# One level of Strassen's scheme in both down-projections of a hybrid decoder layer

## The chip, the core and the metric

The kernel runs on one core of one Trainium2 chip. The metric is device time in microseconds (us) of one execution, the median of several. Engines in the text: PE (TensorE, matmuls; PEld is its weight load), DVE (VectorE), ACT (ScalarE), POOL (GpSimd), SP (SyncE, which issues all the loads and stores here). SBUF is the on-chip memory, PSUM the eight accumulator banks that PE writes.

## What is computed

One decoder layer on 512 tokens of width 1024, in float32. The change lies in the two SwiGLU blocks ("macaron" half-steps), which stand at the start and near the end of the layer:

```
def swiglu(x, w_gu, w_down):
    g, u = jnp.split(x @ w_gu, 2, axis=-1)
    return (jax.nn.silu(g) * u) @ w_down
...
f = swiglu(rms_norm(h, ffn1_pre_g[i]), ffn1_w_gu[i], ffn1_w_down[i])
h = h + 0.5 * rms_norm(f, ffn1_post_g[i])
```

w_gu is 1024 x 5632, w_down 2816 x 1024. Between the blocks stand an attention stage (projection, two mixers, output projection), and after the second one a gate: h + norm(sigmoid(norm(h) @ W_gate) * (p @ W_ple)).

## The kernel before

Every matrix product runs in three terms. An operand X is split into a high part, rounded to the format that PE multiplies (fp32r), and a low part, X minus the high part: `nc.scalar.copy(hi, raw)` on ACT, then a subtraction on DVE (POOL for some weights in the attention stage). A product is then high x high, high x low, low x high: three matmuls of 128 x 128 by 128 x 512.

Stages in order: SwiGLU 1 (22 blocks of gate and up columns, `ffn`, then `down`), the value projection `v_b`, attention with the other projections filled in, the output projection `out_part`, SwiGLU 2, the gate. The order of PE's instructions is the order of the program text; the other engines' instructions are put in order by the planner, which keeps the program's dependencies; `tc.high_priority()` lifts some.

Weights go through a ring of slots (8 KB per partition each: 1024 columns high, 1024 low). `todo` is the list of weights to come, `free` the list of slots; `pump()` hands slots out, `prep` (L131 to L133) loads 512 KB into one of three raw buffers, casts and subtracts; `release(key)`, called where the last matmul on a weight stands, gives the slot back. Four slots lie in `WR`, and up to four more in parts of `HB` that are not written yet. `HB` holds the hidden activations, high and low, 22 blocks of 128 features by 512 tokens. `gu_evac` (L250 to L253) makes one block: silu on ACT, product on DVE, cast on ACT, subtraction on DVE.

`down` goes over 16 of the 22 feature blocks for all four token tiles, 6 matmuls each, and then over the last 6 blocks tile by tile (`M_LAST`), so that tile 0 ends first and its `finish` (norm, residual, norm of the next stage: `post` and `pre`, L193 to L215) runs beside the matmuls of the others. `between(t)` puts the transposes of tiles 0 and 1 into the matmuls of tiles 2 and 3. `extra` prepares the first weights of the next stage (`vb` or `gate`).

Of the kernel before, what the change touches and what calls it, by code (L numbers as in the profile page):

```python
# [22 lines left out]
M_LAST = 6  # L23
# [30 lines left out]
def hybrid_layer(ctx: ExitStack, tc: tile.TileContext, x, p, rel_bias, ffn1_pre_g, ffn1_w_gu, ffn1_w_down,  # L54
# [4 lines left out]
    pool = ctx.enter_context(tc.tile_pool(name="sb", bufs=1))  # L59
    psp = ctx.enter_context(tc.tile_pool(name="ps", bufs=1, space=bass.MemoryType.PSUM))  # L60
# [11 lines left out]
    HB = sb([P, 2, NFF, 512], F32R, "hb")  # L72
    WR = sb([P, 8, 1024], F32R, "wr")
    RAW = sb([P, 3, 1024], F32, "raw")
    FB = sb([P, 7 * 1024], F32, "fb")
# [16 lines left out]
    def mm(o, l, r, start, stop):  # L92
        nc.tensor.matmul(o, l, r, start=start, stop=stop)  # L93
# [3 lines left out]

    def ht(u):
        return (HB[:, 0, 2 * u:2 * u + 2, :].rearrange("p a b -> p (a b)"),
                HB[:, 1, 2 * u:2 * u + 2, :].rearrange("p a b -> p (a b)"))  # L100

    ring = [(WR[:, 2 * i, :], WR[:, 2 * i + 1, :]) for i in range(4)]

# [4 lines left out]
    def source(key):  # L108
# [9 lines left out]
        w = {"d1": ffn1_w_down, "d2": ffn2_w_down, "o": w_out, "gate": w_ple_gate, "ple": w_ple_proj}[kind]  # L118
        return dram(w, i * P * D, [[D, P], [1, D]])

    def prep(key, slot):
        hi, lo = slot
        raw = RAW[:, state["raw"] % 3, :]
# [20 lines left out]
    def release(key):  # L144
        slot = W.pop(key)
        if not any(slot is r for r in retired):
            free.append(slot)
        pump()

# [22 lines left out]

    def flat(a):
        return a.rearrange("p a b -> p (a b)")
# [83 lines left out]
    def down_part(ffn, t, k, slot, w):  # L258
        cols = slice(t * P, (t + 1) * P)
        ps = slot2(slot)  # L260
        xstat([ps[:, 0, :], ps[:, 1, :]], HB[:, 0, k, cols], HB[:, 1, k, cols], w[0], w[1], k == 0, k == NFF - 1)

# [9 lines left out]
    todo += gu_list("1") + [("d1", k) for k in range(NFF)]  # L272


    ring_more = [(ht(7), 11), (ht(8), 13), (ht(9), 15), (ht(10), 17)]
    free.extend(a for a, _ in ring_more[:3])
    praw = FB[:, 6144:7168].rearrange("p (k t c) -> p k t c", k=2, t=NT)
    pT = ht(10)
# [65 lines left out]
    free.append(ring_more[3][0])  # L344
# [4 lines left out]
    def ffn(n, wait_tr, after_first, extra_slots):  # L349
# [7 lines left out]
        for ff in range(NFF):  # L357
            s = gu_slot(ff)
            for slot, until in extra_slots:
                if ff == until:  # L360
                    retired.append(slot)
                    free[:] = [a for a in free if a is not slot]
# [5 lines left out]

    def down(n, extra, finish, between):

        last = NFF - M_LAST
        for k in range(last):
            for t in range(NT):
                down_part(n, t, k, t, W[("d" + n, k)])
            if k == last - 4:
                free.extend([ht(0), ht(1)])
                retired.extend([free[-1], free[-2]])
            release(("d" + n, k))
        extra()
        for t in range(NT):  # L380
            for k in range(last, NFF):
                if k == NFF - 2 and t >= 2:
                    between(t)
                down_part(n, t, k, t, W[("d" + n, k)])
            if t == NT - 1:
                for k in range(last, NFF):
                    release(("d" + n, k))
            finish(t)

# [39 lines left out]
    ffn("1", tr_first, lambda: tables(gu_slot(8), gu_slot(9)), ring_more)  # L429
# [4 lines left out]
    def first_extra():  # L434
        for j in range(4):
            prep(("vb", j), ht(4 + j))
# [33 lines left out]
    VV = HB[:, :, 0:4, :]  # L470

    def vtile(t):
        return HB[:, t % 2, 2 * (t // 2):2 * (t // 2) + 2, :].rearrange("p a (h s c) -> p (a h) s c", s=2, c=64)
# [22 lines left out]
    v_b(0)  # L496
# [7 lines left out]
    MH, ML = HB[:, 0, 6:14, :], HB[:, 1, 6:14, :]  # L504
    VAT = HB[:, 0, 4:6, :].rearrange("p a (b g s c) -> p (a b) g s c", b=2, g=2, s=2)
# [3 lines left out]
    ptb2 = [HB[:, 1, 4, :], HB[:, 1, 5, :]]  # L509
# [4 lines left out]
    def tab(s):  # L514
        if s >= 4:
            return FB[:, 6144 + (s % 2) * 512:6656 + (s % 2) * 512]
        return FB[:, 6144:7168] if s % 2 == 0 else FB[:, 5120:6144]
# [281 lines left out]
    load_tab(5)  # L799
    for s in range(4, 8):  # L800
# [6 lines left out]
        if s == 4:  # L807
            pts[7] = tr_b(*heads_b[7])
        qk_a(s, 1)
# [11 lines left out]
    ring_more = [(ht(7), 11), (ht(9), 15), (ht(8), 13), (ht(10), 17)]  # L821
    prep(("o", 2), ring_more[0][0])
    prep(("o", 3), ring_more[1][0])
# [134 lines left out]
```

## Time and profile before

| | us |
|---|---|
| median of 3 runs | 1018.04 (1015.83 to 1018.29) |
| profiled execution | 1017.18 |
| its span on the core | 1015.4 |
| PE busy | 996.4 |
| DVE busy | 449.7 |
| ACT busy | 377.8 |
| POOL busy | 82.0 |

The span is the time from the first to the last instruction of the profiled execution; 1.8 us lie around it. "Busy" counts the time in which at least one instruction of the engine ran; matmuls overlap, so a busy PE is not PE at its peak.

### The profile page before, as it was taken

What the parts mean: (1) busy time and instruction counts of PE and PEld (TensorE: products, weight loads), DVE (VectorE), ACT (ScalarE), POOL (GpSimd) and SP (SyncE); (2) the same over time, 40 slices, a digit from 0 to 9 for tenths busy, and PEclk for the clock granted to TensorE, in tenths of its full rate; (3) what the DMA queues carried; (4) which work ended last, traced back from release to release, by engine and by line L of the source; (5) the groups of instructions that cost most, each with busy time, mean ns of one, the idle gap of its engine ahead of it and who ended that gap; (6) DMA issues with size and microseconds to landing.
All of it is one profiled execution on the core that took longest, in us unless ns stands there. A gap on an engine that the chain in (4) does not pass through costs nothing.

```text
span 1015.4 us, 12202 instructions
## 1 busy us (share of the span) xinstructions
PE 996.4 (98%) x4889; PEld 840.8 (83%) x4889; DVE 449.7 (44%) x656; ACT 377.8 (37%) x590; POOL 82.0 (8%) x90
## 2 busy tenths in 40 slices
PE   8999999999999999999988999999999999999997
PEld 7988788888888888888877899888888888888886
DVE  4543332232321347267789684333332332233744
ACT  5533232222221234377787454332231231223431
POOL 1000000000000011132232220000000000000211
PEclk9999999999999999999999999999999999999999
DMA  8842533122322455244232375333232223244531
GB/s 291 260 147 87 159 92 104 54 72 83 117 91 104 126 185 187 82 127 123 85 105 63 135 234 172 105 103 104 65 101 63 84 83 125 85 138 151 191 119 63
DMA packets 129715, 123.42 MB, mean 122 GB/s; under 512 B 4361, under 2 KB 110923, under 8 KB 129659
## 3 DMA queue, kind: packets, MB, share of 16 engines
q1 hardware_dynamic: 129659, 122.65, 38.2%
q8 instruction: 38, 0.62, 0.2%
q14 instruction: 18, 0.15, 0.0%
HBM read 109.49 MB, written 10.52 MB: 118 GB/s over the span
## 4 chain that ended last, share of the span: by engine, by line
PE 90%; DVE 5%; ACT 2%; issue 2%; DMA 1%; DVEq 0%; POOL 0%; SPq 0%; POOLq 0%; ACTq 0%
PE banks L93 88%; DVE hb L653 2%; PE banks L224 1%; DVE hb L545 1%; DMA fb<-in_p_dram 1%; DVE fb L689 1%; DVE fb L678 1%; ACT hb L543 0%; ACT hb L552 0%; DVE hb L731 0%; PE banks L616 0%; DVE hb L554 0%; DMA hb<-hb 0%; ACT fb L724 0%; ACT wr L132 0%
## 5 line engine op out<-in xcount | busy, mean ns | idle before, releaser
L93 PE MATMUL banks<-xh,wr 128*128 128x512 f32 (+1 forms) x1152 | 337.8, 373 | 0.0
L93 PE MATMUL banks<-wr,hb 128*128 128x512 f32 x1104 | 257.6, 392 | 0.2 <-DVE hb L731 0.2
L93 PEld LDWEIGHTS banks<-wr,hb 128*128 128x128 f32 x1104 | 208.0, 189 | 43.7 <-DVE hb L731 0.6
L93 PEld LDWEIGHTS banks<-xh,wr 128*128 128x128 f32 x1152 | 210.5, 188 | 37.7 <-issue 0.6
L132 ACT CAST wr<-raw 128x1024 fp32r<-128x1024 f32 x114 | 119.8, 1052 | 318.3 <-PE banks L93 298.9
L93 PE MATMUL banks<-xl,wr 128*128 128x512 f32 (+1 forms) x576 | 214.0, 372 | 0.0
L133 DVE TENSOR_TENSOR wr<-raw,wr 128x1024 fp32r<-128x1024 f32 x100 | 122.1, 1224 | 198.3 <-ACT wr L132 196.0
L93 PE MATMUL banks<-xh,hb 128*128 128x512 f32 (+1 forms) x672 | 184.7, 359 | 0.0
L93 PEld LDWEIGHTS banks<-xh,hb 128*128 128x128 f32 x672 | 120.4, 189 | 18.7
L93 PEld LDWEIGHTS banks<-xl,wr 128*128 128x128 f32 x576 | 108.6, 189 | 18.3
L93 PE MATMUL banks<-xl,hb 128*128 128x512 f32 (+1 forms) x336 | 120.5, 359 | 0.0
L132 ACT CAST hb<-raw 128x1024 fp32r<-128x1024 f32 x54 | 56.6, 1053 | 146.4 <-PE banks L93 95.9
L133 DVE TENSOR_TENSOR hb<-raw,hb 128x1024 fp32r<-128x1024 f32 x50 | 61.0, 1224 | 92.6 <-ACT hb L132 91.4
L251 DVE TENSOR_TENSOR fb<-fb,banks 128x512 f32<-128x512 f32 x44 | 30.3, 688 | 153.8 <-PE banks L93 153.1
L93 PE MATMUL banks<-hb 128*128 128x512 f32 (+3 forms) x440 | 86.7, 344 | 7.6 <-DVE hb L653 7.1
L93 PEld LDWEIGHTS banks<-hb 128*128 128x128 f32 x440 | 70.9, 189 | 20.6 <-DVE hb L653 10.6
L194 POOL TENSOR_SCALAR small<-small 128x1 f32<-128x1 f32 x28 | 12.1, 432 | 779.7 <-ACT fb L193 747.3
L93 PEld LDWEIGHTS banks<-xl,hb 128*128 128x128 f32 x336 | 63.5, 189 | 9.4
L133 POOL TENSOR_TENSOR wr<-raw,wr 128x1024 fp32r<-128x1024 f32 x14 | 34.2, 2446 | 96.4 <-ACT wr L132 96.4
L93 PE MATMUL banks<-hb,xh 128*128 128x512 f32 (+1 forms) x172 | 38.6, 374 | 0.0
L93 PEld LDWEIGHTS banks<-hb,xh 128*128 128x128 f32 x172 | 30.9, 188 | 5.9
L252 ACT CAST hb<-fb 128x512 fp32r<-128x512 f32 x44 | 27.3, 620 | 21.6 <-DVE fb L251 21.6
(102 smaller groups left out, 624.3 us busy)
## 6 DMA issues: line engine op xcount, KB each, us to landing
raw<-in_ffn_w_gu_dram SPq DMA_DIRECT2D x88, 512.0 KB, 3.7
raw<-in_ffn_w_down_dram SPq DMA_DIRECT2D x44, 512.0 KB, 3.2
raw<-in_w_in_dram SPq DMA_DIRECT2D x18, 512.0 KB, 4.3
hd<-fb SPq DMA_DIRECT2D x12, 512.0 KB, 2.6
fb<-hd SPq DMA_DIRECT2D x12, 512.0 KB, 3.6
fb<-in_x_dram SPq DMA_DIRECT2D x8, 512.0 KB, 4.5
raw<-in_w_out_dram SPq DMA_DIRECT2D x8, 512.0 KB, 3.3
raw<-in_w_ple_gate_dram SPq DMA_DIRECT2D x8, 512.0 KB, 3.3
```

Source lines behind the costliest of these rows:

```text
L93: nc.tensor.matmul(o, l, r, start=start, stop=stop)
L132: nc.scalar.copy(hi, raw)
L133: state["lo"].tensor_tensor(lo, raw, f32(hi), op=ALU.subtract)
L194: nc.gpsimd.tensor_scalar(ms, ms, 4 * EPS if half else EPS, None, op0=ALU.add)
L224: nc.tensor.transpose(ps[:, k // 4, (k % 4) * P:(k % 4 + 1) * P], xs[:, k * P:(k + 1) * P], ident)
L251: nc.vector.tensor_tensor(sg, sg, ps[:, 1, :], op=ALU.mult)
L252: nc.scalar.copy(HB[:, 0, ff, :], sg)
L545: nc.vector.scalar_tensor_tensor(q[OWN[1 - j], j, :], PS[OWN[j], bank, :], bfeat[OWN[j], f:f + 1], f32(q[OWN[j], j, :]), op0=ALU.add, op1= ...
L653: nc.vector.tensor_tensor(lo, v, f32(hi), op=ALU.subtract)
L678: nc.vector.tensor_tensor_reduce(out=pi, in0=sview(i)[:, :n], in1=back(tb, 0, n), scale=-0.125, scalar=nsink[:, h:h + 1], op0=ALU.add, op1 ...
L689: nc.vector.tensor_scalar(pi, pi, rs[:, i:i + 1], None, op0=ALU.mult)
```

## The change

Both `down` products are computed by one level of Strassen's scheme. Tokens are halved (0 to 255, 256 to 511), output columns are halved (0 to 511, 512 to 1023), and the 22 feature blocks are taken in 11 pairs, whose two members are the halves of the inner dimension. Of the seven products, four (m1, m2, m4, m5) are accumulated over all pairs in a first pass, each in a quarter of PSUM; ACT and DVE then combine the banks, and three (m3, m6, m7) are added in a second pass over all pairs. A product has 2 token tiles x 3 terms = 6 matmuls of 512 columns per pair. The last three pairs of the second pass are kept back and done tile by tile.

The sums and differences of blocks that the products need are made on chip, pair by pair: first pass "a" (two blocks of w_down as they are), "b" (two sums), "A" (token operands, from the hidden block); second pass "c" and "e" (three sums) and "B" (token operands). The sums are POOL instructions (`add`), the split into high and low (`cut`) one ACT and one DVE instruction. Each pass loads w_down, so it is read twice; a load is now a pair, 1 MB, into half of a raw buffer that has grown from 3 to 4 rows. The hidden activations are kept once, in float32 (`cur["t"]`); what held the low half is five more slots of the ring and the place of one extra "e" operand, so there are nine slots for `down`. `gu_evac` loses the cast and the subtraction.

The core of the diff:

```diff
+NPAIR, LAST = 11, 3
+GROUPS = [(0, 1), (2, 3), (4, 5), (6, 7), (8,), (9, 10)]
...
+    def cut(src, hi, lo):
+        nc.scalar.copy(hi, src)
+        nc.vector.tensor_tensor(lo, src, f32(hi), op=ALU.subtract)
+
+    def pair_load(n, m):
+        q = (state["raw"] + 1) // 2 * 2
+        state["raw"] = q + 2
+        raw = RAW[:, q % 4:q % 4 + 2, :]
+        w = ffn1_w_down if n == "1" else ffn2_w_down
+        nc.sync.dma_start(raw, dram(w, 2 * m * P * D, [[D, P], [P * D, 2], [1, D]]))
+        return raw.rearrange("p a b -> p (a b)")
...
+        tb = FB[:, (m % 2) * 1024:(m % 2 + 1) * 1024]
+        add = nc.gpsimd.tensor_tensor
+        if kind == "a":
+            raw = state["pair"] = pair_load(n, m)
+            cut(halves(raw, 0, 1536), two(hi), two(lo))
+        elif kind == "b":
+            raw = state["pair"]
+            add(tb[:, 0:512], raw[:, b11], raw[:, b22], op=ALU.add)
+            add(tb[:, 512:1024], raw[:, b21], raw[:, b11], op=ALU.subtract)
+            cut(tb, hi, lo)
+        elif kind == "A":
+            h = flat(cur["t"])[:, m * 1024:(m + 1) * 1024]
+            ta = FB[:, 2048:2816] if m % 2 == 0 else FB[:, 3072:3840]
+            add(ta[:, 0:512], h[:, 0:512], h[:, 512:1024], op=ALU.add)
+            add(ta[:, 512:768], h[:, 0:256], h[:, 768:1024], op=ALU.add)
+            cut(h[:, 768:1024], hi[:, 768:1024], lo[:, 768:1024])
+            cut(ta, hi[:, 0:768], lo[:, 0:768])
+            mid = two(h[:, 256:768])
+            nc.vector.tensor_tensor(mid, mid, halves(h, 0, 768, w=256), op=ALU.subtract)
+        elif kind == "c":
+            raw = pair_load(n, m)
...
+            td = FB[:, 4096 + (m % 2) * 512:4608 + (m % 2) * 512]
+            add(tb[:, 0:512], raw[:, b12], raw[:, b22], op=ALU.subtract)
+            add(tb[:, 512:1024], raw[:, b11], raw[:, b12], op=ALU.add)
+            add(td, raw[:, b21], raw[:, b22], op=ALU.add)
+            cut(tb, hi, lo)
+            cut(td, eh, el)
+        elif kind == "B":
+            cut(flat(cur["t"])[:, m * 1024:m * 1024 + 768], hi[:, 0:768], lo[:, 0:768])
...
     def gu_evac(ffn, ff, slot):
         ps = slot2(slot)
-        sg = FB[:, 6144 + (ff % 2) * 512:6144 + (ff % 2 + 1) * 512]
-        nc.scalar.activation(sg, ps[:, 0, :], AF.Silu)
-        nc.vector.tensor_tensor(sg, sg, ps[:, 1, :], op=ALU.mult)
-        nc.scalar.copy(HB[:, 0, ff, :], sg)
-        nc.vector.tensor_tensor(HB[:, 1, ff, :], sg, f32(HB[:, 0, ff, :]), op=ALU.subtract)
+        h = cur["t"][:, ff, :]
+        nc.scalar.activation(h, ps[:, 0, :], AF.Silu)
+        nc.vector.tensor_tensor(h, h, ps[:, 1, :], op=ALU.mult)
...
+    def product(bank, i, x, xc, y, yc, start, stop):
+        (xh, xl), (yh, yl) = x, y
+        xs, ys = slice(xc + i * P, xc + (i + 1) * P), slice(yc, yc + 512)
+        mm(bank[i], xh[:, xs], yh[:, ys], start, False, True)
+        mm(bank[i], xh[:, xs], yl[:, ys], False, False, True)
+        mm(bank[i], xl[:, xs], yh[:, ys], False, stop, True)
...
     def down(n, extra, finish, between):
...
+        for m in range(NPAIR):
+            s, e = m == 0, m == NPAIR - 1
+            wa, wb, x = (W[(k + n, m)] for k in "abA")
...
+                for i in range(2):
+                    m4(i), m5(i)
+                for i in range(2):
+                    m2(i), m1(i)
+            for k in "abA":
+                release((k + n, m))
...
+        with tc.high_priority():
+            for i in range(2):
+                nc.scalar.copy(q[i], C12[i])
+                nc.vector.tensor_tensor(q[i], C22[i], q[i], op=ALU.subtract)
+            for i in range(2):
+                nc.vector.tensor_tensor(C22[i], q[i], C21[i], op=ALU.subtract)
+            for i in range(2):
+                nc.scalar.copy(r[i], C11[i])
+                nc.vector.tensor_tensor(C11[i], q[i], C11[i], op=ALU.add)
+            for i in range(2):
+                nc.vector.tensor_tensor(C21[i], C21[i], r[i], op=ALU.add)
...
+        for f in (m3, m6, m7):
+            for m in range(3):
+                f(m, 0), f(m, 1)
+        for m in range(3):
+            done(m)
+        for m in range(3, NPAIR - LAST):
+            for f in (m3, m6, m7):
+                f(m, 0), f(m, 1)
+            done(m)
         extra()
+        last = range(NPAIR - LAST, NPAIR)
+        for t in range(2):
+            for f in (m3, m7):
+                for m in last:
+                    f(m, t, m == NPAIR - 1)
+            with tc.high_priority():
+                nc.scalar.copy(q[t], C12[t])
+                nc.vector.tensor_tensor(C22[t], C22[t], q[t], op=ALU.add)
             finish(t)
+        for t in range(2):
+            for m in last:
+                if t == 1 and m == NPAIR - 1:
+                    between(2)
+                m6(m, t, m == NPAIR - 1)
...
+            finish(2 + t)
```

The rest moves buffers about. Tile 1's transposes go from `down` into `v_b(0)` and into the first half of the gate's tile 0. `extra` prepares four `vb` or five `gate` weights at the start of the last three pairs. The second SwiGLU begins with one free slot where it had two, and gets three more when the output projection has ended.

## Rows read from the trace of the kernel before

**Rows 1.** The page, parts 1 and 2: busy us (share), instructions; busy tenths in 40 slices.
```profile
PE 996.4 (98%) x4889; PEld 840.8 (83%) x4889; DVE 449.7 (44%) x656; ACT 377.8 (37%) x590; POOL 82.0 (8%) x90
...
PE   8999999999999999999988999999999999999997
...
POOL 1000000000000011132232220000000000000211
PEclk9999999999999999999999999999999999999999
```

**Rows 2.** The chain of waits in order of time: start us, us, what.
```profile
104.11 274.05 PE banks L93 x1206
378.16 0.87 PE banks L224 x8
...
611.64 338.58 PE banks L93 x1584
```

**Rows 3.** Timeline (start us, us, engine, line), start and end of the first down-projection.
```profile
269.19 30.99 PE L93 MATMUL banks<-wr,hb 128*128 128x512 f32 x136
...
390.87 1.03 ACT L193 ACTIVATE fb<-banks 128x1024 f32<-128x1024 f32 x1 [0.26 <-PE banks L93]
```

**Rows 4.** Stretches: us, busy us (instructions) of PE PEld DVE ACT POOL; clock, DMA share, GB/s.
```profile
9.00:20.00 11.00, 11.00 (x43) 8.94 (x42) 4.58 (x6) 6.54 (x9) 1.59 (x4) 1.00 1.08 334
...
269.20:390.90 121.70, 121.70 (x547) 100.94 (x546) 43.36 (x38) 36.11 (x44) 5.15 (x12) 1.00 0.37 126
...
512.00:531.00 19.00, 15.88 (x93) 13.38 (x92) 16.21 (x49) 15.95 (x40) 9.50 (x4) 1.00 0.44 140
```

**Rows 5.** Groups by line and form: count, busy us, mean ns, idle before.
```profile
L133 DVE TENSOR_TENSOR wr<-raw,wr 128x1024 fp32r<-128x1024 f32 x100 | 122.1, 1224 | 198.3 <-ACT wr L132 196.0
...
L132 ACT CAST wr<-raw 128x1024 fp32r<-128x1024 f32 x114 | 119.8, 1052 | 318.3 <-PE banks L93 298.9 <-issue 4.6 <-DMA raw<-in_ffn_w_down_dram 4.4
...
L253 DVE TENSOR_TENSOR hb<-fb,hb 128x512 fp32r<-128x512 f32 x44 | 30.1, 684 | 2.7 <-ACT hb L252 2.7
...
L653 DVE TENSOR_TENSOR hb<-banks,hb 128x768 fp32r<-128x768 f32 x4 | 3.8, 954 | 1.3 <-ACT hb L652 1.2
...
L653 DVE TENSOR_TENSOR hb<-banks,hb 128x256 fp32r<-128x256 f32 x8 | 3.4, 425 | 0.9 <-ACT hb L652 0.7
```

**Rows 6.** Single lines: durations ns min/median/max, first and last start us.
```profile
L133 POOL TENSOR_TENSOR wr<-raw,wr x14: 2395/2409/2620, 420.8 to 537.3; 128x1024 fp32r<-128x1024 f32 x14
L133 POOL TENSOR_TENSOR hb<-raw,hb x4: 2397/2414/2830, 518.9 to 552.0; 128x1024 fp32r<-128x1024 f32 x4
...
L194 POOL TENSOR_SCALAR small<-small x28: 222/224/1317, 12.1 to 968.3; 128x1 f32<-128x1 f32 x28
...
L195 POOL TENSOR_TENSOR small<-small,neghalf x28: 568/569/1575, 12.4 to 968.7; 128x1 f32<-128x1 f32 x28
```

**Rows 7.** The timeline of DVE and POOL in the attention stage.
```profile
518.89 4.77 POOL L133 TENSOR_TENSOR hb<-raw,hb 128x1024 fp32r<-128x1024 f32 x2 [4.64 <-ACT hb L132]
...
522.72 1.22 DVE L653 TENSOR_TENSOR hb<-banks,hb 128x1024 fp32r<-128x1024 f32 x1
...
536.29 0.69 DVE L731 TENSOR_TENSOR hb<-fb,hb 128x512 fp32r<-128x512 f32 x1
...
549.67 2.40 POOL L133 TENSOR_TENSOR hb<-raw,hb 128x1024 fp32r<-128x1024 f32 x1 [10.00 <-PE banks L93]
...
549.86 2.76 DVE L731 TENSOR_TENSOR hb<-fb,hb 128x512 fp32r<-128x512 f32 x1
```

**Rows 8.** The timeline of one token tile, end of the second down-projection.
```profile
944.81 1.03 ACT L193 ACTIVATE fb<-banks 128x1024 f32<-128x1024 f32 x1 [0.79 <-PE banks L93]
...
951.00 1.28 DVE L206 SCALAR_TENSOR_TENSOR fb<-fb,small,bc 128x1024 f32<-128x1024 f32 x1 [2.18 <-POOL small L195]
```

**Rows 9.** Loads of the down weights, 512 KB each.
```profile
DMA to landing us min/median/max: 3.0/3.2/4.2
```

More of the change, by code (lines that the diff above doesn't have):

```diff
@@ new lines, in cut, with operand @@
+    def cut(src, hi, lo):
[8 more added lines that the diff above has]
+        return raw.rearrange("p a b -> p (a b)")
+    def operand(key, slot):
+        kind, n, m = key[0][0], key[0][1], key[1]
+        hi, lo = slot
+        b11, b12, b21, b22 = (slice(i * 512, (i + 1) * 512) for i in range(4))
+        tb = FB[:, (m % 2) * 1024:(m % 2 + 1) * 1024]
[19 more added lines that the diff above has]
+            raw = pair_load(n, m)
+            g = next(i for i, x in enumerate(GROUPS) if m in x)
+            if len(GROUPS[g]) == 1:
+                W[("e" + n, g)] = state["spare"][:, 0:512], state["spare"][:, 512:1024]
+            eh, el = (a[:, GROUPS[g].index(m) * 512:][:, :512] for a in W[("e" + n, g)])
+            td = FB[:, 4096 + (m % 2) * 512:4608 + (m % 2) * 512]
[6 more added lines that the diff above has]
+            cut(flat(cur["t"])[:, m * 1024:m * 1024 + 768], hi[:, 0:768], lo[:, 0:768])
+        W[key] = slot
@@ L121, in prep @@
     def prep(key, slot):
+        if key[0][0] in "abAceB" and len(key[0]) == 2 and key[0] != "vb":
+            return operand(key, slot)
         hi, lo = slot
-        raw = RAW[:, state["raw"] % 3, :]
+        raw = RAW[:, state["raw"] % 4, :]
         state["raw"] += 1
@@ L145, in release, with gone, retire @@
         slot = W.pop(key)
-        if not any(slot is r for r in retired):
+        if any(slot is r for r in retired):
+            gone(slot)
+        else:
             free.append(slot)
         pump()
+    gone_slots, after = [], []
+    def gone(slot):
+        gone_slots.append(slot)
+        for need, more in list(after):
+            if all(any(x is g for g in gone_slots) for x in need):
+                after.remove((need, more))
+                free.append(more)
+    def retire(slot):
+        retired.append(slot)
+        if any(slot is f for f in free):
+            free[:] = [f for f in free if f is not slot]
+            gone(slot)
     def kview(slot, k):
@@ L270, in gu_list, with down_list @@
         return [(kind + ffn, ff) for ff in range(NFF) for kind in "gu"]
[L272 to L278, printed above, removed]
+    def down_list(n):
+        keys = []
+        for m in range(NPAIR):
+            keys += [("a" + n, m), ("b" + n, m), ("A" + n, m)]
+        for m in range(NPAIR):
+            keys += [("e" + n, g) for g, x in enumerate(GROUPS) if x[0] == m and len(x) > 1]
+            keys += [("c" + n, m), ("B" + n, m)]
+        return keys
+    todo += gu_list("1") + down_list("1")
+    slots1 = [half_slot(h1, j) for j in range(5)]
+    state["spare"] = h1[:, 10240:11264]
+    free.extend(slots1[:3])
+    praw = FB[:, 5632:6656].rearrange("p (k t c) -> p k t c", k=2, t=NT)
+    pT = half_slot(h1, 4)
     def load_p(k):
@@ L367, in ffn @@
                 after_first()
-    def down(n, extra, finish, between):
[L371 to L378, printed above, removed]
-        extra()
[L380 to L387, printed above, removed]
-            finish(t)
+    C11, C12 = [PS[:, 2 * i, :] for i in range(2)], [PS[:, 2 * i + 1, :] for i in range(2)]
@@ L833, in hybrid_layer @@
     state["lo"] = nc.vector
-    todo.extend(gu_list("2") + [("d2", k) for k in range(NFF)])
-    free.extend(a for a, _ in ring_more[2:])
+    todo.extend(gu_list("2") + down_list("2"))
+    free.append((flat(H1[:, 16:18, :]), flat(H1[:, 20:22, :])))
+    after.append((o23, (flat(H1[:, 14:16, :]), flat(H1[:, 18:20, :]))))
     pump()
@@ L862, in tr_second @@
             transpose_x(t, xss.pop(t), wslot[t])
-    ffn("2", tr_second, lambda: None, ring_more)
+    free.extend(half_slot(h1, j) for j in range(3))
+    state["spare"] = h1[:, 6144:7168]
+    pump()
+    lower(F32, "hidden2")
+    ffn("2", tr_second, lambda: None)
     g_post = bcast(0, ffn2_post_g)
@@ L870, in last_extra @@
     def last_extra():
-        for k in range(6):
-            prep(("gate", k), ht(2 + k))
-        todo.extend([("gate", 6), ("gate", 7)])
+        assert not todo
+        lower(F32R, "gates")
+        for k in range(5):
+            prep(("gate", k), half_slot(flat(cur["t"]), k))
+        todo.extend([("gate", k) for k in range(5, 8)])
     xss, xbuf = {}, {}
@@ L885, in hybrid_layer @@
     ybuf = [xbuf[1], xbuf[1], xbuf[2], xbuf[3]]
-    es = [FB[:, 6144:7168], RAW[:, 0, :], RAW[:, 1, :], RAW[:, 2, :]]
+    es = [RAW[:, i, :] for i in range(NT)]
     for t in range(NT):
```

113 lines of the change are left out of this document (77 added, 36 removed).

## The prediction, made before the changed kernel was run

> **What bounds the kernel now.** I read the page first: TensorE (PE) is busy 98% of the span, only the last slice falls below eight tenths, and the granted clock is full in every slice [rows 1]. Then the chain of waits in order of time: two unbroken runs of matmuls, 274 us and 339 us long, cover both SwiGLUs but for their ends [rows 2]. So in the stages that the change touches the time is the count of matmuls times their pitch, and nothing that VectorE (DVE), ScalarE (ACT), GpSimd (POOL) or the loads do there ends late. The first down-projection runs from 269.19 to 390.87 [rows 3]; taking out its two sets of transposes (0.87 us each [rows 2]) leaves 119.9 us for 22 x 4 x 6 = 528 matmuls: 0.2271 us each. In that stretch DVE was busy 43.4 us of 121.7, ACT 36.1, POOL 5.2, and the loads ran at 126 GB/s [rows 4]. All have room, but the room was measured with POOL almost idle.
>
> **What the change removes.** Seven block products, 11 pairs of row blocks, 2 token tiles and 3 terms make 462 matmuls for 528. Two projections save 132 x 0.2271 = 30.0 us. This term is certain; the question is what the operands cost. In gu_evac a cast and a subtraction per block go as well (L252, L253); PE never waited for them, so that is worth nothing.
>
> **What it adds, per pair.** PE now takes 24 x 0.2271 = 5.45 us for a pair in the first pass and 18 x 0.2271 = 4.09 us in the second. The operands of that pair must come in the same time.
>
> DVE, first pass: subtractions of 1024 (a), 1024 (b), 768 and 256 columns (A), and the in-place difference of 512. By the nearest rows of these widths 1.224 + 1.224 + 0.954 + 0.425 + 0.684 = 4.51 us. Second pass: 1024 and 512 (c), 768 (B): 1.224 + 0.684 + 0.954 = 2.86 us [rows 5]. ACT casts the same columns at 1.05 us per 1024 [rows 5], about 3.3 and 2.5 us: it fits under PE.
>
> POOL, first pass: adds of 512, 512 (b), 512 and 256 (A); second: three of 512 (c). The trace has adds of 1024 alone, 2.41 us. The 512 lies between half of that, 1.20, and 0.57 + (2.41 - 0.57)/2 = 1.49, if the fixed part is that of the 128x1 power. I take the 0.22 us of the plainer 128x1 addition as the fixed part: 1.315 us, and 0.77 for 256 [rows 6]. That is 4.71 us for the first pass and 3.95 for the second.
>
> Each engine alone would fit under PE. But every added DVE operation reads two SBUF operands, and so does every POOL add. What happens when two such meet stands in the attention stage [rows 7]: a POOL subtraction started at 549.67 and took its usual 2.40 us to 552.07; a DVE subtraction of 512 (L731) started at 549.86, took 0.69 us elsewhere, and here took 2.76, to 552.62. It stood until POOL had finished and then ran for 0.55 us; the next POOL subtraction took 2.83 us instead of 2.41 [rows 6]. A DVE subtraction with one operand in PSUM (L653), beside another POOL run, took its usual 1.22 us [rows 7]. So the two take turns, and their times add: 4.51 + 4.71 = 9.2 us per pair in the first pass, 2.86 + 3.95 = 6.8 in the second, against 5.45 and 4.09 on PE. Of the whole duration the turn hid 0.68 - 0.55 = 0.13 us. With 9 and 6 operations per pair the sums fall to 8.05 and 6.03 if every turn hides that much. Not every operation follows one of the other engine, so I take the middle, 8.6 and 6.4.
>
> [...] By the whole instruction, 9.2 and 6.8, the result would be about 1103 us; with every turn hiding 0.13 it would be about 1066.
>
> **The sum for one down-projection**, from its first matmul:
> - Head start. The nine slots are handed out as gate and up weights are released, so at time 0 they hold all operands of pairs 0 and 1 and most of pair 2; what pair 2 lacks is A's DVE work, 0.954 + 0.425 + 0.684 = 2.06 us. POOL's adds of pair 3 need no slot and may be done: 4.71 us less.
> - First pass: the operands of the last pair are there at 8 x 8.6 + 2.06 - 4.71 = 66.2 us.
> - Second pass: 11 x 6.4 = 70.4 us more. DVE also has six combinations of banks (6 x 0.684 = 4.1 us [rows 5]). Each has a PSUM operand, so POOL may run beside them: 0 to 4.1, I take 2.05. The last pair's operands are there at 138.6. PE's own wait for the combinations is covered by the 18 matmuls of m3.
> - Tail: of the 54 matmuls kept for last 6 can run before; 48 x 0.2271 = 10.9 us. End at 149.5, against 119.9 before: +29.6 us, twice +59.2.
>
> **The seams.** Token tile 0 used to have 60 matmuls between its end and the transposes that need it; now it has 33, 7.5 us. Its way from the first square to the normalised tile took 944.81 to 952.28, 7.5 us [rows 8]. In front come a copy and an addition of 512 (0.6 + 0.7), so it is 1.3 us late at least, and 6.2 if four weight subtractions of 1.22 us stand ahead in DVE's queue, as the vb and gate loads now fall into the same 12 us; 0 to 0.7 us follows for the evacuation before the next matmul. I take 3.5 us per projection. The second SwiGLU begins with one weight slot fewer prepared: 0 to 2.7 us (24 matmuls of half width), I take 1. Together 8 us. Tables, attention and the end of the layer keep their work: nothing.
>
> The bytes double: 1 MB per pair. In the forecast that is 1 MB in 6.4 us, 164 GB/s; 334 GB/s was moved for 11 us early on [rows 4]. A load of 0.5 MB landed in 3.2 us [rows 9], so one of 1 MB in about 3.2 + 0.5 MB / 334 GB/s = 4.8 us. It then holds its half of the buffer through the adds, in turns, 6.8 us: (4.8 + 6.8) / 2 = 5.8 us per pair, under 6.4. So the loads set nothing.
>
> Against the profiled execution's 1017.2 us (0.9 under the median): 1017.2 + 59.2 + 8 = **1084 us**. Its ends: POOL at 1.20 with every turn hiding 0.13, no combinations, seams of 1.3: 1043. POOL at 1.49 with nothing hidden, 4.1, 6.9 and 2.7: 1138.
>
> **Rivals.**
> - *Faster: the two engines pass each other.* If POOL's adds and DVE's subtractions overlap (the meeting in rows 7 was peculiar to it), each engine fits, and the time is 1017.2 - 30.0 + 8 = 995 us. In the second pass the raw buffer then sets (4.8 + 3.95)/2 = 4.4 us per pair, 0.3 over PE: 8 pairs, twice, 5 us, so 995 to 1000. It decides where the sum per pair falls below PE's 5.45 and 4.09. For it: the 43 us of DVE seen before are far from full. Against it: the same two operations in the same form stood for each other. Chance 0.09.
> - *The clock falls too.* PE would wait about 3 us in each pair. In this trace it was at most two tenths idle in a stretch (512 to 531), with the granted clock still full [rows 4], so no row shows what longer waits do. [...] Chance 0.08. [...]
> - *The turns are mostly hidden*: the head start is larger than the slots say, and supply just meets PE. 1005 to 1030 us. Chance 0.03.
>
> **How the numbers follow.** Forecast 0.80, rivals 0.09, 0.08, 0.03. The forecast's own range, 1043 to 1138, with half of the clock case, gives 1035 to 1145: outside lie 0.09, 0.03, half of 0.08 and about 0.03 of the forecast itself. 0.3% is about what a measurement of this kernel can tell from no change. Faster by more has 0.09 and a third of the last rival, 0.10; within it 0.02; slower 0.88.
>
> **What would show it.** In the changed trace: 462 matmuls per projection; PE idle for some 3 us a pair, waiting for casts or subtractions of operands from about the fourth pair on; POOL and DVE busy nearly end to end, with durations of 512-wide POOL adds well over 1.3 us and of 1024-wide DVE subtractions well over 1.22, the excess of each ending where the other's operation ends. The first pass lasting some 71 us and the second some 78. I am wrong if DVE's subtractions keep 1.22 us beside POOL's adds, if PE shows no gaps in the projections, or if PE's gaps end on a load.

## The result and the profile after

The changed kernel took 1086.52 us (median of 4 runs, 1082.47 to 1086.69) against 1018.02 for the kernel before on the same chip: ratio 1.0668 (95% interval 1.064 to 1.0697). The profiled execution took 1086.63 us with a span of 1084.2. The forecast was 1084, slower.

The page of the changed kernel, parts 1 and 2 (busy us, share of the span, instructions; then busy tenths in 40 slices), which answers to [rows 1]:

```profile
PE 1006.8 (93%) x4757; PEld 836.9 (77%) x4757; DVE 636.7 (59%) x764; ACT 433.8 (40%) x668; POOL 344.9 (32%) x244
...
PE   8999999999987976999988999999999999877697
...
POOL 1010000033788853132232211100002338799311
PEclk9999999999997988999999999999999999979699
```

132 matmuls are gone, but PE was busy for 10.4 us longer and idle for 58.4 us longer (1084.2 - 1006.8 = 77.4, against 1015.4 - 996.4 = 19.0). At the old pitch the busy time should have fallen by the 30.0 us of the prediction, so the matmuls that are left took 40.4 us more. That is the whole account: -30.0 + 58.4 + 40.4 = +68.8 us of span. The slices show where: PE falls to seven and six tenths in the two down-projections, where POOL is busy, lowest in the slice at the end of each, and the granted clock falls to eight, seven or six tenths in most of these slices (not in the one from 976 to 1003 us).

The stretches by stage say the same in us. First the kernel before, then the changed one; each has the first down-projection up to the last transposes of the `vb` stage, the work up to the second down-projection, and that projection up to the last transposes of the gate. Columns: us, busy us (instructions) of PE, PEld, DVE, ACT, POOL; granted clock, DMA share, GB/s.

```profile
269.20:407.10 137.90, 137.90 (x626) 114.53 (x625) 54.74 (x51) 41.97 (x53) 6.73 (x16) 1.00 0.42 138
407.10:841.20 434.10, 426.09 (x2181) 361.81 (x2180) 223.17 (x413) 193.70 (x348) 57.03 (x34) 1.00 0.36 108
841.20:990.10 148.90, 148.90 (x674) 123.63 (x674) 59.95 (x59) 47.46 (x64) 10.14 (x22) 1.00 0.39 134
```

```profile
268.20:438.00 169.80, 139.54 (x560) 109.62 (x559) 147.88 (x115) 75.94 (x105) 115.06 (x75) 0.90 0.54 180
438.00:879.30 441.30, 431.47 (x2181) 366.70 (x2180) 224.72 (x404) 188.01 (x336) 79.37 (x52) 0.99 0.35 107
879.30:1058.80 179.50, 153.11 (x608) 120.53 (x607) 152.63 (x123) 80.98 (x116) 118.92 (x81) 0.88 0.49 173
```

The three stages grew by 31.9, 7.2 and 30.6 us. In the first, PE used to be busy without a gap; now it idles for 30.3 us, and its matmuls take 139.5 us where 137.9 - 15.0 = 122.9 would do at the old pitch. DVE was busy for 148 us where it had been for 55, and POOL for 115 where it had been for 7, in one stretch of 170 us.

Why PE waits, in the steady part of the first pass. The timeline of POOL (start us, us, engine, line, operation, count; in brackets the idle time before, and what ended it):

```profile
300.18 2.20 POOL L176 TENSOR_TENSOR fb<-hidden 128x512 f32<-128x512 f32 x1 [0.89 <-DVE wr L147]
302.33 0.92 POOL L177 TENSOR_TENSOR fb<-hidden 128x256 f32<-128x256 f32 x1
303.40 1.56 POOL L170 TENSOR_TENSOR fb<-raw 128x512 f32<-128x512 f32 x1
304.92 2.27 POOL L171 TENSOR_TENSOR fb<-raw 128x512 f32<-128x512 f32 x1
308.08 2.19 POOL L176 TENSOR_TENSOR fb<-hidden 128x512 f32<-128x512 f32 x1 [0.89 <-DVE hb L147]
```

and DVE's in the same stretch:

```profile
301.15 1.50 DVE L147 TENSOR_TENSOR hb<-hidden,hb 128x256 fp32r<-128x256 f32 x1
302.58 1.22 DVE L181 TENSOR_TENSOR hidden<-hidden 128x512 f32<-128x512 f32 x1
303.73 2.32 DVE L147 TENSOR_TENSOR hb<-raw,hb 128x1024 fp32r<-128x1024 f32 x1
305.96 3.17 DVE L147 TENSOR_TENSOR hb<-fb,hb 128x768 fp32r<-128x768 f32 x2
```

DVE has hardly a gap, yet most of its time is standing: a subtraction of 256 columns takes 1.50 us for 0.42, one of 512 takes 1.22 for 0.68, one of 1024 takes 2.32 for 1.22 [rows 5]. POOL's adds of 512 take up to 2.27 us; the shortest of them took 1.26, those of 256 at least 0.73. Take the last add of the pair: it starts at 304.92, DVE's 1024 ends at 306.05, 1.13 us later, and the add ends another 1.14 us after that, at 307.19. So each stands for most of the other. One pair takes 308.08 - 300.18 = 7.9 us, and PE needs 5.45.

PE's timeline in the first pass and at the end of that projection, answering to [rows 3]:

```profile
309.19 7.08 PE L95 MATMUL banks<-hb 128*128 128x512 f32 x23 [2.18 <-DVE hb L147]
...
317.07 5.51 PE L95 MATMUL banks<-hb,wr 128*128 128x512 f32 x23 [0.58 <-DVE hb L147]
...
324.98 7.11 PE L95 MATMUL banks<-wr 128*128 128x512 f32 x23 [2.17 <-DVE wr L147]
331.93 5.60 PE L95 MATMUL banks<-hb 128*128 128x512 f32 x24
339.85 2.93 PE L95 MATMUL banks<-hb,wr 128*128 128x512 f32 x6 [2.32 <-ACT fb L497]
...
414.64 1.97 PE L318 MATMUL banks<-ident,fb 128*128 128x128 f32 x8 [8.41 <-DVE fb L300]
416.26 1.63 PE L95 MATMUL banks<-hb,wr 128*128 128x512 f32 x3
420.20 4.00 PE L95 MATMUL banks<-heads,xh 128*128 128x512 f32 x16 [2.31 <-DVE xl L325]
```

PE starts a pair every 7.9 us, waiting for a subtraction. Two things more are to be seen. After a wait of 2.2 us the 23 matmuls took 7.08 us instead of some 5.4. And the longest wait is not for an operand of the product at all: PE stands 8.41 us for the normalised row tile (`fb`, L300) that its transposes need. The waits of PE over the whole execution (us in total, times, longest) put numbers to it:

```profile
PE banks L318 <- DVE fb L300: 17.3, 3, 8.4
PE banks L95 <- DVE hb L147: 10.9, 7, 2.6
PE banks L95 <- DVE wr L147: 10.0, 5, 2.5
PE banks L95 <- ACT wr L146: 8.5, 4, 2.8
...
PE banks L95 <- ACT fb L497: 4.6, 2, 2.3
PE banks L95 <- ACT hb L146: 4.4, 2, 2.7
PE banks L95 <- DVE xl L325: 2.9, 2, 2.3
```

Operands of the products (L146, L147) cost PE 33.8 us, row tiles (L318, and `xl`) 20.2; neither had a wait in the kernel before (its largest was 7.1 us in all for `hb`, L653, in the attention stage).

### The profile page after: what moved, and what is told of

Read it like the earlier page. It is cut to its first block, busy times and chain, and to the rows that moved or that the text cites. A ratio compares the mean times of both kernels' runs of the same rounds, so it can differ in the third digit from the quotient of the medians.

```text
span 1084.2 us, 12403 instructions
## 1 busy us (share of the span) xinstructions
PE 1006.8 (93%) x4757; PEld 836.9 (77%) x4757; DVE 636.7 (59%) x764; ACT 433.8 (40%) x668; POOL 344.9 (32%) x244
## 4 chain that ended last, share of the span: by engine, by line
PE 66%; DVE 14%; POOL 6%; issue 5%; DMA 5%; ACT 3%; DVEq 0%; SPq 0%; POOLq 0%; ACTq 0%
PE banks L95 64%; DVE hb L147 4%; DVE wr L147 4%; POOL fb L189 2%; POOL fb L190 2%; DMA raw<-in_ffn_w_down_dram 2%; DVE hb L826 1%; PE banks L318 1%; POOL fb L191 1%; DMA fb<-in_p_dram 1%; DVE fb L862 1%; DMA fb<-in_x_dram 1%; DVE fb L851 1%; DMA raw<-in_w_in_dram 0%; DMA raw<-in_ffn_w_gu_dram 0%
## 5 line engine op out<-in xcount | busy, mean ns | idle before, releaser
L95 PE MATMUL banks<-xh,wr 128*128 128x512 f32 (+1 forms) x944 | 274.6, 371 | 0.0
L95 PE MATMUL banks<-xh,hb 128*128 128x512 f32 (+1 forms) x880 | 249.2, 367 | 0.0
L211 ACT CAST wr<-raw 128x1024 fp32r<-128x1024 f32 x60 | 63.1, 1053 | 137.8 <-PE banks L95 110.2
L95 PE MATMUL banks<-hb 128*128 128x512 f32 (+2 forms) x354 | 96.8, 407 | 10.3 <-DVE hb L147 5.3
L212 DVE TENSOR_TENSOR wr<-raw,wr 128x1024 fp32r<-128x1024 f32 x46 | 57.2, 1246 | 67.3 <-ACT wr L211 65.8
L147 DVE TENSOR_TENSOR hb<-fb,hb 128x1024 fp32r<-128x1024 f32 (+2 forms) x46 | 70.5, 1549 | 27.2 <-ACT hb L146 27.1
L95 PE MATMUL banks<-hb,wr 128*128 128x512 f32 x258 | 72.5, 429 | 13.4 <-ACT wr L146 5.7
L95 PE MATMUL banks<-wr 128*128 128x512 f32 x264 | 70.9, 422 | 10.3 <-DVE wr L147 7.5
L147 DVE TENSOR_TENSOR wr<-fb,wr 128x1024 fp32r<-128x1024 f32 (+2 forms) x42 | 64.6, 1555 | 19.4 <-ACT wr L146 19.2
L95 PEld LDWEIGHTS banks<-hb,wr 128*128 128x128 f32 x258 | 52.5, 207 | 28.7 <-ACT wr L146 6.9
```

Source lines behind the costliest of these rows:

```text
L95: nc.tensor.matmul(o, l, r, start=start, stop=stop, skip_group_check=loose)
L147: nc.vector.tensor_tensor(lo, src, f32(hi), op=ALU.subtract)
```

## The experiments

Two theories stood against each other. **Turns:** a POOL add and a DVE subtraction whose operands all lie in SBUF stand for each other, so their times add up. **The rivals:** the operands are late for another reason (POOL is simply too slow, the loads, the combinations of banks), or the time goes at the ends of the projections. An edit is shown against the changed kernel unless it says before.

**No adds at all.** The sums are left out; the casts and subtractions take raw and hidden blocks directly.

```diff
-            add(tb[:, 0:512], raw[:, b11], raw[:, b22], op=ALU.add)
-            add(tb[:, 512:1024], raw[:, b21], raw[:, b11], op=ALU.subtract)
-            cut(tb, hi, lo)
+            cut(raw[:, 0:1024], hi, lo)
...
-            add(td, raw[:, b21], raw[:, b22], op=ALU.add)
...
+            cut(raw[:, b22], eh, el)
```

> The changed kernel without POOL's adds: each operand is cut straight from the loaded block or the hidden block, so the sums of Strassen's scheme are left out; matmuls, loads, casts and DVE subtractions keep their number and shape. Theory (POOL's adds and DVE's subtractions take turns): DVE's subtractions are back at 1.22 us per 1024, each pair's operands take 4.5 and 2.9 us, under PE's 5.45 and 4.09, so both projections run at PE's pace but for their seams: 985 to 1005 us, against 1086. Rival (the second load of the weights, the two halves of the raw buffer or the nine slots set the pace): these are all unchanged, so 1060 to 1090 us.

Measured: 1028.75 us, ratio 1.0121 (1.0092 to 1.015). Neither range. The adds are worth 1086.5 - 1028.8 = 58 us; but the kernel without them is still some 41 us above the 987 to 988 that 30 us fewer matmuls should give. In this kernel the first pass runs at PE's own pace, a pair every 5.44 us. Its page has PE busy for 980.9 of 1027.2 us: 14.5 us of slower matmuls and 27.3 us of waits more than before, and those are

```profile
PE banks L308 <- DVE fb L290: 19.8, 3, 8.7
...
PE banks L95 <- DVE xl L315: 3.2, 2, 2.6
```

row tiles again. So there are two causes, and the second has nothing to do with the adds.

**The adds on DVE.** One engine, so no turns between two:

```diff
-        add = nc.gpsimd.tensor_tensor
+        add = nc.vector.tensor_tensor
```

> The changed kernel with the adds on DVE in place of POOL, otherwise the same. Theory of turns: an add costs 0.68 us on DVE where it held the other engine up for some 1.25 us on POOL; per pair DVE has 4.51 + 2.47 = 7.0 and 2.86 + 2.05 = 4.9 us, some 6.4 and 4.5 as consecutive operations overlap, against 7.9 and 5.8 measured with both engines. First pass about at PE's pace, second a little over it: 1020 to 1050 us, most likely 1035. Rival (POOL and DVE work side by side, and something else, loads or slots, sets the pace): DVE now carries more than PE's 5.45 us per pair alone, so no gain: 1086 us or more.

Measured: 1041.89 us, ratio 1.0243 (1.0218 to 1.0268), as expected. Giving DVE all the work is 45 us faster than sharing it with an engine that was free. An add of 512 takes 0.69 us there and a subtraction of 1024 takes 1.22 again. The durations of a pair add up to 7.0 and 4.9 us, and a pair of the first pass came every 6.2 us (two subtractions of a pair's loaded block start at 296.72 and 302.94). That is more than PE's 5.45 and less than the 7.9 of the shared way. PE still ran the first pass without a wait, which fits the operands that are ready at its start.

**POOL writes but doesn't read.** In the place of each add POOL fills the same columns twice.

```diff
-        add = nc.gpsimd.tensor_tensor
+        def add(out, in0, in1, op):
+            nc.gpsimd.memset(out, 0.0)
+            nc.gpsimd.memset(out, 1.0)
```

> The changed kernel with each POOL add replaced by two POOL fills of the same columns (so the sums are left out): POOL stays in the chain of every operand, ACT and DVE wait for it as before, but it reads nothing from SBUF. Theory of turns, if it is POOL's reading that meets DVE's second operand: DVE's subtractions stay at 1.22 us, 985 to 1010 us, as without the adds. Rival 1 (any POOL instruction that touches SBUF takes a turn): DVE's subtractions are stretched by the length of a fill, 1010 to 1060 us. Rival 2 (the wait for POOL as a link of the chain, not a meeting with DVE, sets the pace): about as much POOL time as before, so over 1050 us.

Measured: 1028.86 us, ratio 1.0122 (1.0093 to 1.0151), the same as without adds and, like that run, outside the 985 to 1010. It lies in the range of rival 1, but the sign of that rival, stretched subtractions, is missing. Groups by line and form (count, busy us, mean ns, idle before), and one source line (ns min/median/max):

```profile
L167 POOL MEMSET fb<- 128x512 f32 x132 | 67.0, 528 | 0.5
```

```profile
L147 DVE TENSOR_TENSOR hb<-fb,hb x46: 684/1219/1226, 244.9 to 944.3; 128x1024 fp32r<-128x1024 f32 x27, 128x512 fp32r<-128x512 f32 x12, 128x768 fp32r<-128x768 f32 x7
```

POOL is busy for 2 x 0.53 = 1.06 us where an add takes 1.26, the waits between the engines are all there, and no subtraction of the operands took over 1.227 us. Work and waits on POOL cost nothing here; its reading does.

**DVE reads one operand.** Each subtraction becomes a sum over the same columns; the low parts are left out, and the high parts stand in for them on PE.

```diff
-        nc.vector.tensor_tensor(lo, src, f32(hi), op=ALU.subtract)
+        nc.vector.reduce_sum(JUNK[:, 0:2] if len(src.shape) == 3 else JUNK[:, 0:1], src, axis=mybir.AxisListType.X)
...
-            mid = two(h[:, 256:768])
-            nc.vector.tensor_tensor(mid, mid, halves(h, 0, 768, w=256), op=ALU.subtract)
+            nc.vector.reduce_sum(JUNK[:, 0:1], h[:, 256:768], axis=mybir.AxisListType.X)
...
```

> The changed kernel with POOL's adds as they are, but each DVE subtraction of the operands replaced by a DVE sum over the same columns: as many columns at one SBUF operand, the result a single number (the low parts are left out, the high part stands in their place in the matmuls). Theory of turns between POOL's reading and DVE's second operand: DVE's operations stay at their own length and POOL's adds fall to 1.25 to 1.35 us; the projections run at PE's pace as in the runs without adds or with fills, 1028.8 us: 1018 to 1040. Rival (any DVE operation beside a POOL add takes a turn, or the bandwidth of SBUF is shared): POOL's adds stay near 1.8 us, 1055 to 1087 us.

Measured: 1021.69 us, ratio 1.0051 (1.0032 to 1.0071), as expected. POOL's adds are untouched, and yet (groups by line and form):

```profile
L148 DVE TENSOR_REDUCE junk<-fb 128x1 f32<-128x1024 f32 x44 | 53.7, 1220 | 49.5 <-POOL fb L190 25.7 <-POOL fb L172 23.4
...
L190 POOL TENSOR_TENSOR fb<-raw 128x512 f32<-128x512 f32 x22 | 28.5, 1297 | 0.0
```

against these two in the changed kernel:

```profile
L190 POOL TENSOR_TENSOR fb<-raw 128x512 f32<-128x512 f32 x22 | 41.9, 1906 | 0.0
L147 DVE TENSOR_TENSOR hb<-raw,hb 128x1024 fp32r<-128x1024 f32 x14 | 24.7, 1767 | 6.0 <-ACT hb L146 5.7
```

The four kernels close the square: POOL reads and DVE reads two, 1086.5; POOL only writes, 1028.9; DVE reads one, 1021.7; no adds, 1028.8. Only both together cost that much. That the third is 7 us under the last isn't explained. The sum over columns also writes next to nothing, so this run alone can't tell the second operand from the write; in [rows 7] a DVE subtraction with one operand in PSUM wrote its 1024 columns beside POOL at its usual 1.22 us.

**The adds of the second pass alone left out**, by the part of the first edit that stands under "c":

> The changed kernel without POOL's adds in the second pass alone (its sums are left out); the first pass keeps its adds. Theory of turns: the first pass stays at some 69 us, 7.9 us per pair; the second, 55 us in the changed kernel from the end of the first to the last pair's operands, falls to PE's pace, some 35 us: 20 us twice, so 1040 to 1055 us. With the run without any adds at 1028.8, the first pass then accounts for the remaining 15 to 20 us. Rival (the gain without adds came from the first pass, the second being held by its 1 MB loads in 4 us): 1070 us or more, with PE's waits in the second pass ending on loads.

Measured: 1053.33 us, ratio 1.0363 (1.0339 to 1.0387), as expected. Taken out first, the second pass's adds give back 33 us; the first pass's are then worth the other 1053.3 - 1028.8 = 25, where 15 to 20 were expected. The price of 58 us lies in both passes, as the two sums per pair had it.

**Two and four idle adds in the kernel before**, per block of `w_down`, into a buffer that nobody reads. The products are as they were. The edit is shown against the kernel before, with two adds.

```diff
...
+        if key[0] in ("d1", "d2"):
+            for j in range(2):
+                nc.gpsimd.tensor_tensor(JUNK, raw[:, 0:512], raw[:, 512:1024], op=ALU.add)
```

> The kernel before, with two POOL adds of 512 columns per down-projection weight row block, reading the loaded block and writing columns that nobody reads. Theory of turns: some of DVE's subtractions in the projections last up to 1.1 us longer, but per block of 5.45 us of matmuls POOL and DVE need 2 x 1.27 + 1.22 = 3.8 us in turns, so no change: 1014 to 1021 us. Rival (a meeting costs more than the other's duration, or holds up PE or the loads too): over 1022 us.

> As the run with two adds, but four per block. Theory of turns: 4 x 1.27 + 1.22 = 6.3 us per block, less some 0.3 us hidden at the turns, against 5.45 us on PE: the projections become supply-bound by 0.5 to 0.9 us per block once the head start of some eight slots is used up, 5 to 15 us each: 1025 to 1048 us. Rival (POOL and DVE pass each other): POOL alone needs 5.1 us per block, under PE: 1014 to 1021 us.

Measured: 1018.07 us (ratio 1.0024, 1.0009 to 1.004) with two, 1054.42 us (1.037, 1.0353 to 1.0387) with four, against 1016.17 for the kernel before on that chip. Two adds cost some 2 us, and the interval lies just above 1; they do meet subtractions: one source line of DVE, ns min/median/max,

```profile
L134 DVE TENSOR_TENSOR wr<-raw,wr x100: 1210/1225/2329, 7.0 to 970.0; 128x1024 fp32r<-128x1024 f32 x100
```

A block gives PE 5.45 us; DVE's 1.22 and two adds of 1.26 make 3.7. With four it is 1.22 + 4 x 1.26 = 6.3, and POOL runs without a break at

```profile
299.83 26.15 POOL L137 TENSOR_TENSOR junk<-raw 128x512 f32<-128x512 f32 x16
```

26.15 / 4 = 6.5 us a block. Five subtractions fell into that stretch, since DVE still went at PE's pace, and 16 x 1.26 + 5 x 1.22 = 26.3: the times add, and next to nothing is hidden. At this pace 22 x (6.5 - 5.45) = 23 us per projection would be lost; (1054.42 - 1016.17) / 2 = 19 were. Operands that the slots hold ready at the start may be the difference; that isn't shown. The time came out 6 us over its range.

Nobody waits for these sums, so the loss took another way. PE kept its pace in the first projection up to 357 us and then waited 15.3 us in all, 10.8 of them at once, for the cast of a weight (waits of PE over the execution; then the chain before that wait's end):

```profile
PE banks L94 <- ACT wr L133: 21.4, 2, 10.8
```

```profile
362.65 2.16 POOL junk L137
...
370.18 3.50 DMA raw<-in_w_in_dram
```

POOL had fallen behind and still held a raw buffer, and the load into that buffer stood in front. So the sum of both engines against PE's pace decides, as in the prediction, and the change's own buffers, loads and order aren't needed for such a loss.

**Low parts of the next stage's weights left out.** Now the second cause. `extra` prepares `vb` or `gate` weights, and their subtractions stand in DVE's queue before the row tiles. The timeline of the changed kernel at the end of the first projection (DVE and SP, which issues the loads):

```profile
395.04 4.63 DVE L212 TENSOR_TENSOR heads<-raw,heads 128x1024 fp32r<-128x1024 f32 x4 [1.11 <-ACT heads L211]
...
399.59 0.69 DVE L546 TENSOR_TENSOR banks<-banks,fb 128x512 f32<-128x512 f32 x1
...
402.69 1.23 DVE L212 TENSOR_TENSOR wr<-raw,wr 128x1024 fp32r<-128x1024 f32 x1 [1.28 <-ACT wr L211]
403.83 0.69 DVE L546 TENSOR_TENSOR banks<-banks,fb 128x512 f32<-128x512 f32 x1
...
404.55 0.45 SPq L294 DMA_DIRECT2D fb<-in_x_dram  x1
...
410.91 2.48 DVE L309 SCALAR_TENSOR_TENSOR fb<-fb,small 128x1024 f32<-128x1024 f32 x2 [1.80 <-DMA fb<-in_x_dram]
...
413.31 1.28 DVE L300 SCALAR_TENSOR_TENSOR fb<-fb,small,bc 128x1024 f32<-128x1024 f32 x1
```

Four weight subtractions stand before the addition that completes tile 0 (L546), and a fifth, which waits for its cast, before that of tile 1. Only when tile 1's is done is its load of x issued, at 404.55. Tile 0's norm (L300), for which PE waits, then stands in the queue behind the residuals of later tiles (L309), and these wait for that load.

```diff
+        if key[0] in ("vb", "gate"):
+            W[key] = hi, hi
+            return
```

> The changed kernel without the DVE subtraction for the value weights and the gate weights that are prepared beside the last three pairs (their low part is left out; the high part stands in its place). Theory: these four and eight subtractions stand in DVE's queue ahead of the norms of the ending token tiles, so PE's two waits for the transposes, 8.4 and 6.7 us, fall to 0 to 4 us each; 1070 to 1080 us. Rival (the late load of the residual rows alone makes the wait): PE's waits stay over 6 us each, 1083 to 1088 us.

Measured: 1078.0 us, ratio 1.0606 (1.0574 to 1.0637), as expected: 8.5 us. PE's wait for the transposes' row tiles fell from 17.3 to

```profile
PE banks L321 <- DVE fb L303: 7.5, 3, 3.3
```

The wait for `xl` rose from 2.9 to 5.9 us, so row tiles cost 13.4 us in place of 20.2.

**Rows of x earlier.** `cnt["h"]` chooses the buffers of the row tiles. With another start value the loads don't wait for a buffer that the combination of banks holds.

```diff
+    cnt["h"] = 6
     down("1", first_extra, finish1, between_parts)
...
+    cnt["h"] = 12
     down("2", last_extra, finish2, between_parts)
```

> The changed kernel with the buffers of the residual rows counted on by two, so that in the first projection tile 1's row no longer waits for the buffer that the bank combination uses; nothing else. Theory: PE's wait of 8.4 us for tile 0's transposes ends on a norm that stands in DVE's queue behind tile 1's, which waits for that row; it falls to 3 to 5 us, and the time by 2 to 6 us, to 1080 to 1085. Rival (the four weight subtractions ahead in DVE's queue set that wait alone): 1085 to 1088 us.

Measured: 1083.46 us, ratio 1.0665 (1.0631 to 1.0699): no difference that can be told. The wait went from 8.41 to 6.52 us only, where 3 to 5 were expected. With the adds on DVE as well it was 1039.1 us, ratio 1.0218 (1.0184 to 1.0252), again not to be told from the 1041.89 without it:

> Both together: adds on DVE (1041.9 us alone) and the buffers of the residual rows counted on. Theory: the two gains add, 1035 to 1041 us. It stays above the kernel before (1016 to 1018 us), since the ends of the projections and the second pass on DVE remain. Rival (with the supply faster the late row is hidden or the norm's place in DVE's queue decides): no gain, 1041 to 1044 us.

So the loads of x have some part in the wait, and the weight subtractions in DVE's queue the larger one. This was the best version that does all of the work, and it doesn't beat the kernel before.

**No adds, and both edits to the ends:**

> The run without adds (1028.8 us), and besides without the low part of the value and gate weights that are prepared beside the last three pairs (the high part stands in its place), and with the buffers of the residual rows counted on so that tile 1's row does not wait for a buffer of the projection's own. What is left out: the sums and those low parts. Theory: what keeps the run without adds above the 987 us of the saved matmuls alone is DVE's queue and late rows at the ends of the projections; PE's three waits for transposes, 19.8 us together, fall under 8 us: 1008 to 1018 us. Rival (it is spread over the rest, the clock or the loads): 1024 us or more.

Measured: 1015.56 us, ratio 0.9994 (0.998 to 1.0007), as expected, though the waits for transposes fell to 9.5 us and not under 8. Even with adds that cost nothing and weights that aren't fully made, the 30 us of matmuls bring no time. The page has PE busy for 977.4 us of 1013.7: 11.0 us of slower matmuls and 17.3 us of waits more than before. The waits are mostly

```profile
PE banks L311 <- DVE fb L293: 9.5, 3, 3.9
...
PE banks L95 <- DVE xl L318: 5.5, 2, 3.4
```

15.0 of the 17.3 us. Of the 41 us that the first experiment left open, the two edits account for 13, and the rest is 15 us of row tiles, some 2 of other waits and 11 of slower matmuls.

## Why the prediction was right

The total was 2.5 us off. The main step held: the two engines take turns, the times of their operations add, and the sum per pair exceeds PE's time. That the total came so near is luck: the projections themselves were put 20 us too high, and their ends and the stages between 23 us too low.

- **What is removed:** 4889 to 4757 matmul instructions, 132 fewer; 30.0 us at the old pitch. Right.
- **Turns:** right, and shown from four sides above. The durations were near: 1.26 to 1.28 us for POOL's 512 against 1.315, and 0.73 for 256 against 0.77. DVE's own were exact (0.42, 0.68, 0.95, 1.22).
- **"I take the middle, 8.6 and 6.4": the step that failed.** It was 7.9 and 5.6 us a pair (5.6 is the mean of ten pairs, from the first add at 329.57 to the one at 385.51). With the measured durations the sums are 4.51 + 3 x 1.27 + 0.73 = 9.05 and 2.86 + 3 x 1.27 = 6.67. So 9 operations hid 1.15 us, 0.13 each; 6 hid 1.07, at least 0.18 each, since the combinations of banks lie in these pairs too. On the average each hid at least what the single row had shown, and the lower end of the sum was the value to take. The reason given for the middle, that not every operation follows one of the other engine, didn't hold: with all adds on DVE, where each operation follows one of its own engine, a pair took 6.2 us for durations of 7.0, so 9 operations hid some 0.8 us.
- **Supply:** with 7.9 and 5.6 the same working gives 8 x 7.9 + 2.06 - 4.54 = 60.7 us for the last pair of the first pass and 60.7 + 61.6 + 2.05 = 124.4 for the second. Measured were 61.3 (the last subtraction of that pair ended at 329.49; PE, still in the pair before at a granted clock of 0.75, came to it at 331.93) and 125.7 (393.94). So the head start was right; the prediction's own 66.2 and 138.6 were 5 and 13 us too late. The share of the combinations isn't tested by this, since the 5.6 has them in it; there were eight of them, 5.5 us, and not six.
- **The signs:** "from about the fourth pair on" doesn't follow from the prediction's own sum: by it the operands of the fourth pair are there at 8.6 + 2.06 - 4.71 = 6 us, when PE needs them at 16, and PE catches up at the eighth. It did, at 309.19, and waited 2.2, 0.6 and 2.2 us and not some 3.
- **The tail and the end of the projection:** from the last operand to the end, without the transposes and their wait, PE took 417.7 - 393.9 - 1.6 - 8.4 = 13.8 us for 10.9 (the last matmul starts at 417.26, 0.43 us after the one before); its first 9 matmuls, from 392.81 to 397.14, took twice their pitch, 0.48 us each at a granted clock of 0.50. The first projection took, counted in the same way, 417.7 - 268.2 - 1.6 - 8.4 = 139.5 us against 119.9: +19.6, where +29.6 was forecast. The second took +19.1. Together 39 for 59.
- **The seams: the other step that failed,** 3.5 us per projection. From the end of supply and tail the first stage lost 31.9 - 19.6 = 12.3 us more: 8.4 by the wait of the transposes, 2.3 by that for `xl`, and 1.6 that go with matmuls and transposes at the lower clock (0.50 from 414.64 to 416.60, 0.73 from 416.3 to 420.2); the second 30.6 - 19.1 = 11.5. The mechanism was named (33 matmuls of cover for a path of 7.5 us, weight subtractions ahead in DVE's queue), and then I took 3.5 out of 1.3 to 6.9. The queue was at its worst, the load of x came on top, and the path then had a second end, the low part of the tile.
- **"PE's own wait for the combinations is covered by the 18 matmuls of m3":** it was not; PE waited 2.32 us for the first copy (`ACT fb L497`). It cost nothing that can be seen, since the supply was later still.
- **"Tables, attention and the end of the layer keep their work: nothing":** the middle stage took 7.2 us more for the same instructions. From 438.0 to 595.8 it was 157.8 us for 155.1, with no more waiting than before (7.6 us for 8.0) but slower matmuls (granted clock 0.91 from 560 to 596). The start of the second SwiGLU took 53.2 us for 49.4, and PE did not wait for a weight: 2.2 us for a row tile, 1.6 for slower matmuls (granted clock 0.88 from 638 to 652). But the chain to that row tile runs through a load of gate and up weights (5.26 us from 633.51) and their subtraction in DVE's queue. The forecast was 1 us for both together, put down to a weight slot.
- **Loads set nothing:** nearly right. The 1 MB loads landed in 4.7 us, as estimated (4.8), and PE had no wait on one. But the chain has four of them, one in the first projection and three in the second (at 925.07, 944.32 and 965.59). Each was issued when its half of the buffer came free, and the subtraction or add that needed it came next; what this cost can't be told apart. The first of them (chain: start us, us, what):

```profile
313.98 4.70 DMA raw<-in_ffn_w_down_dram
```

- **The rival of the clock** came true in part: the mean granted clock was 0.956 for 0.999, and 0.90 and 0.88 in the two stages. The range of 1035 to 1145 us has half of that case in it, at a price that no run shows; what the runs showed is 40.4 us of slower matmuls, in a time within 2.5 us of the forecast. Slower matmuls may have filled waits for operands. How much of the 40.4 us of slower matmuls moved the end can't be read from these runs, since none keeps the waits and the clock apart; that stays open, and with it the split of the loss at the ends. By the slices of the page the clock was at six to eight tenths in five of the seven slices in which PE was busy for seven tenths or less, and at nine or more in all others.

Which share is which, then: the turns cost 58 us by experiment; the ends cost at least 13 by experiment, and 15 more of waits for row tiles remain in the trace of the last run. The 30 us that the change saves are less than either sum, the 58 of the turns or the 41 of the ends and the clock.

## What to carry to other kernels

An engine that is free by the page was not free for work that met another engine's operands (POOL, busy 8% of the span before; its adds cost 58 us): add the two streams' durations and compare the sum with PE's time for the same piece. Well below it the work was nearly free here (two adds a block, 3.7 us for 5.45: 1018.07 us against 1016.17), above it the excess was paid but for a head start (four, 6.3: 1054.42). Where the two streams alternate, 0.13 to 0.18 us came off for each operation; with four adds to one subtraction nearly nothing did. If the sum is too large, the same adds on DVE alone may be cheaper (here 1041.89 us against 1086.52). And where a change takes matmuls out of the end of a stage, count what stands in the other engines' queues at that point in its worst order: those matmuls were the cover of the next stage's row tiles.

## What was not expected of the hardware

A short wait was followed by matmuls at a lower clock. After 2.18 us without work, the stretch from 309.2 to 316.2 had a granted clock of 0.76:

```profile
309.20:316.20 7.00, 7.00 (x24) 5.59 (x24) 7.00 (x5) 2.88 (x4) 6.11 (x5) 0.76 0.26 98
```

The kernel before had a stretch with more idle time, 512 to 531, at the full clock [rows 4]. So one such row at full clock did not show that the next wait of that size would be free of it. The transposes show it too: eight took 1.03 us in an unbroken run (436.98 to 438.02, granted clock 1.00) and 1.97 after the wait of 8.41 us (414.64 to 416.60, granted clock 0.50).
